# Layer 2 of a hybrid trunk: merge gates and merge products as separate units, and retention's first q and k between the grouped-query projections

## The chip, the cores and the metric

The kernel runs on one core of a Trainium2 chip. The metric is the device time of one execution in microseconds (us). Of three runs of the kernel before, the median is 1741.61 us (1741.46 to 1746.81). The engines are named PE (TensorE), DVE (VectorE), ACT (ScalarE), POOL (GpSimd) and SP (SyncE, which issues the DMAs).

## The reference

A trunk of two layers works on 512 latent tokens `x` and 256 context tokens `y`, 1024 channels wide. In each layer three branches read the same normalized input, each branch is gated, and a merge adds them up. Cut to what matters:

```python
def hybrid_layer(x, y, ..., need_ctx):                     # need_ctx only in layer 1
    hx = rms_norm(x, norm_w) * (1 + scale_x) + shift_x     # hy likewise
    rq, rk, rv, rg, nq, nk, nv, ng, gq, gk, gv, gg, mg = split_cols(hx @ w_in)
    # retention, 4 heads of 128, both directions, v used after its mean is taken off
    ret_x = head_group_norm(bidir_retention(...), ret_gn_w) * silu(rg)
    # neighbourhood attention, 8 heads of 64, windows of 8 rows x 16 columns, plus context keys
    na_x = neighbourhood_attention(...) * silu(ng)
    # grouped-query attention, 8 query heads on 2 key heads, rms norm and rope on q and k
    gqa_x = gqa_blocks(axial_rope(rms_norm(gq)), k_all, v_all) * silu(gg)
    g_ret, g_na, g_gqa = split(sigmoid(mg), 3)             # the merge gates, 1024 wide each
    m = g_ret * (ret_x @ w_ret_o) + g_na * (na_x @ w_na_o) + g_gqa * (gqa_x @ w_gqa_o)
    x = x + gate_x * (m @ w_out)
```

The same is done for the context in layer 1 alone. After layer 2 comes a last rms norm of `x`.

## The kernel before, in words

Everything is held transposed: channels on partitions, tokens along the free axis. Each fp32 operand is split into a high part and the remainder, so a product is three matmuls (`mm3`, L277 to L280): high by high, remainder by high, high by remainder. Normalized input is `hxh`, `hxl`, weights are `whi`, `wlo`. Weights arrive in tiles of 512 KB: `_load` (L252) issues the DMA to `raw` on SP, ACT casts each half to `whi` (L262), POOL subtracts it to get `wlo` (L264). The order of tiles is the list `stream`, filled from the plan at L1236.

A projection unit (`u_proj`) for one 128-wide block of output channels is 24 matmuls of 512 columns in layer 2 (8 input tiles by 3), and for units that also need the context tokens 24 more of 256 columns. `u_tok` makes v with tokens on partitions: 144 matmuls of 256 columns.

PE's order is written by hand. A `Unit` is a generator that emits one `mm3` per step. `run` emits units whole. `window` (L113) emits a branch's attention steps, and after each step as many `mm3` of filler units as the step's weight asks for; what is left over runs at the end of the window or, with `keep`, later. `defer(us, fn)` puts a small PE step (a transpose, a column sum) off until that many estimated microseconds of PE work have been emitted. The other engines are ordered by a scheduler that works from the same program; within an engine instructions run strictly in that order. PSUM is split into banks by tag: `pj` 2 (projections), `s` 2 (scores), `pt` 3 (transposes), `pv` 1.

One layer runs through these stages:

- Neighbourhood attention (NA) in four windows `p`, two heads each. Per head: four score steps (L595, L596, evicted by DVE with the bias, exponential on ACT, normalized by DVE and POOL), six transpose steps (L624; ACT casts the high part `ph`, L438, and DVE subtracts for `pl`, L439), six `pv` steps (L635 with `ph`, L636 with `pl`). Fillers are the next window's q and k and the window's gate `u_g`. Window 3 has no next window, so its filler is one gate alone.
- The intro to grouped-query attention (GQA): `u_k`, `u_v`, `u_q(0)`, merge 0 of the NA branch. k takes squares, a column sum (L225, L226), a wide inverse square root in three rounds of DVE and ACT (L218 to L220), a rope of four DVE instructions (L704 to L707), and ACT casts it to `gk` (L767). v is copied by ACT to `sg` (L779, 512 and then 256 tokens) and transposed on PE (L784).
- GQA in four windows `p`. Per window four units (two heads by two halves of the queries) of four score steps (L851, L852; DVE evicts to `p`, L853), exponential on ACT (L862), normalization by DVE and POOL (L867), three transpose steps (L875) and three `pv` steps (L887). Fillers: gate, next q, and merges 1 to 7 as listed in `GA`. The next q needs transposes of its squares `gsq` (L725), sums of them (L726), and a rope.
- The intro to retention (RET): tables `dt`, `E`, `C` by DVE and ACT, then `u_qk(0,"q")`, `u_qk(0,"k")`, `u_v(0)`, whose evictions take DVE four instructions per third (L990 to L996).
- RET in four windows, with merges of the GQA branch as fillers; then the merges of the RET branch and the out projection.

A merge for output block `d` (`u_merge`) is one unit: gate projection of 24 matmuls, a tanh on ACT into `mt`, then a product of 12 matmuls with the branch's gated output `gat`, which DVE multiplies into `m[d]` (L1104).

Of the kernel before, what the change touches and what calls it, by code (L numbers as in the profile page):

```python
# [20 lines left out]
NX = 512  # L21
# [18 lines left out]
def trunk_kernel(ctx: ExitStack, tc: tile.TileContext, xt, wcol, wv, adaw, wbr, wout, nabias, vecs,  # L40
# [197 lines left out]
    SQ = 100  # L238
    KLAG = 3.0
    Q0LAG = 2.0  # L240
# [251 lines left out]
    class NA:  # L492
# [189 lines left out]
    class GQA:  # L682
# [19 lines left out]
        def rope(self, t):  # L702
            sh = self.ap.tile([128, NX], F32, tag="sh", name="sh", bufs=1)
            nc.vector.stream_shuffle(out=sh, in_=t[:, :NX], mask=[(i + 16) % 32 for i in range(32)])  # L704
            nc.vector.tensor_tensor(t[:, :NX], t[:, :NX], self.cs[:, 0], op=ALU.mult)
            nc.vector.tensor_tensor(sh, sh, self.cs[:, 1], op=ALU.mult)
            nc.vector.tensor_tensor(t[:, :NX], t[:, :NX], sh, op=ALU.add)  # L707

        def stats_evac(self, t, w, ntok, done, lag):

            st = {}

            def ev(ps, o, n):
                if o == 0:
                    st["ss"] = self.ap.tile([128, 12], F32, tag="qss", name="qss", bufs=2)
                ss = st["ss"]
                sq = self.ap.tile([128, 512], F32, tag="sh", name="gsq", bufs=1)
                with tc.high_priority(SQ):
                    nc.scalar.activation(sq[:, :n], ps, AF.Square)
                nc.scalar.activation(t()[:, o:o + n], ps, AF.Copy, scale=w)  # L720

                def one():
                    pt = bank("pt")
                    for i in range(n // 128):
                        nc.tensor.transpose(pt[:, 128 * i:128 * i + 128], sq[:, 128 * i:128 * i + 128], ident)  # L725
                    nc.vector.tensor_reduce(ss[:, o // 64:(o + n) // 64], pt[:, :n].rearrange("p (t c) -> p t c", c=64),  # L726
                                            axis=AX.X, op=ALU.add)
                    if o + n == ntok:
                        done(ss[:, :ntok // 64])
                defer(lag, one)  # L730
            return ev

        def u_k(self):
            st = {}

            def ev(ps, o, n):
                ap = self.ap
                if o == 0:
                    st["kr"] = ap.tile([128, NT], F32, tag="qr", name="kr", bufs=1)
# [5 lines left out]
                sq = ap.tile([128, 512], F32, tag="sh", name="gsq", bufs=1)  # L745
                sh, sl = a[:, 0, c].bitcast(F32R), a[:, 1, c].bitcast(F32R)
# [6 lines left out]
                def one():  # L753
# [18 lines left out]
        def u_v(self):  # L772
            st = {}

            def ev(ps, o, n):
                if o == 0:
                    st["v"] = self.ap.tile([128, NT], F32, tag="sg", name="sg", bufs=1)
                vf = st["v"]
                nc.scalar.copy(vf[:, o:o + n], ps)  # L779

                def tr():
                    pt = bank("s")
                    for i in range(n // 128):
                        nc.tensor.transpose(pt[:, 128 * i:128 * i + 128], vf[:, o + 128 * i:o + 128 * i + 128], ident)  # L784
                    for i in range(n // 128):
                        v = self.V[:, o // 128 + i]
                        src = pt[:, 128 * i:128 * i + 128].rearrange("p (h d) -> p h d", h=2)
                        nc.scalar.copy(v[:, :, 0:64], src)
                        nc.vector.tensor_tensor(v[:, :, 64:128], src, f(v[:, :, 0:64]), op=ALU.subtract)
                defer(1.5, tr)  # L790
            return u_proj(ap_wcol[self.l][CT_GV], G_ALL, ev)

        def u_q(self, p):
            def get():
                if p not in self.qr:
                    self.qr[p] = self.ap.tile([128, NT], F32, tag="qr", name="qr", bufs=1)
                return self.qr[p]
# [124 lines left out]
    class RET:  # L922
        def __init__(self, l, g):
            self.l, self.g = l, g
            self.nq = NT if l == 0 else NX
            self.gq = G_ALL if l == 0 else G_LAT
            self.ot, self.sg = {}, {}

        def open(self):
# [33 lines left out]
        def u_qk(self, h, which):  # L963
            sc = 1.0 if which == "q" else float(np.float32(128.0) ** np.float32(-0.5))

            def ev(ps, o, n):
                if o == 0:
                    t = (self.ap.tile([128, NT], F32R, tag=which + "h", name=which + "h", bufs=1),
                         self.ap.tile([128, NT], F32R, tag=which + "l", name=which + "l", bufs=1))
                    setattr(self, which, t)  # L970
# [8 lines left out]
        def u_v(self, h):  # L979
            def ev(ps, tp):  # L980
                ap = self.ap
                if tp == 0:
# [93 lines left out]

    def u_merge(l, b, d, g, m, getpool):
        gq = G_ALL if l == 0 else G_LAT
        nq = NT if l == 0 else NX
        src = [ap_wcol[l][CT_MG + 8 * b + d]]  # L1080
        if d % 2 == 0:
            src.append(ap_wbr[l][b][d // 2])

        def gen(ws):
            if d % 2 == 0:
                wbr_now[0] = ws[1]
            t = getpool().tile([128, nq], F32, tag="mt", name="mt", bufs=1)

            def ev(ps, o, n):
                nc.scalar.activation(t[:, o:o + n], ps, AF.Tanh, scale=0.5)  # L1090
            yield from g_proj(ws[0], gq, ev)
            hi, lo = wbr_now[0][d % 2]
            if len(g) < 4:
                due(True)
            for o, n in gq:
                ps = bank("pj")
                for k in range(4):
# [10 lines left out]
                    yield 3 * n * NS  # L1108
        return Unit(nq * 36 * NS, src, gen)

    wbr_now = [None]

# [5 lines left out]
    def start_phase(na, first):  # L1118
# [47 lines left out]
    for l in range(DEPTH):  # L1166
# [30 lines left out]
        def open_m(l=l, m=m, mtp=mtp):  # L1197
# [3 lines left out]
            for d in range(8):  # L1201
                m[d] = mp.tile([128, nq], F32, tag="m", name="m", bufs=8)
            mtp["cm"] = pool(f"mt{l}")
            mtp["p"] = mtp["cm"].__enter__()
        do(open_m)
        do(gqa.open)
        mg = lambda b, d, g: u_merge(l, b, d, g, m, lambda mtp=mtp: mtp["p"])
        runs(gqa.u_k(), gqa.u_v(), gqa.u_q(0))
        MA = ((0, 1), (2, 3), (4, 5), (6, 7))
        GA = ((1, 2), (3, 4), (5,), (6, 7))  # L1210
        old = []
        for p in range(4):
            if p == 0:
                runs(mg(BR_NA, 0, g_na))
            do(lambda gqa=gqa, p=p: (due(True), gqa.split_q(p)))
            us = [gqa.u_g(p)] + ([gqa.u_q(p + 1)] if p < 3 else []) + [mg(BR_NA, d, g_na) for d in GA[p]]
            win(lambda gqa=gqa, p=p: gqa.steps(p), us, GLEAD, GKEEP[l][p], old)
# [6 lines left out]
        do(lambda ret=ret: ret.tables(0))  # L1224
        runs(ret.u_qk(0, "q"), ret.u_qk(0, "k"), ret.u_v(0))
        for h in range(4):
            us = [ret.u_g(h)] + [mg(BR_GQA, d, g_gq) for d in MA[h]]
# [4 lines left out]
        do(lambda ret=ret: (due(True), ret.close()))  # L1232
        plan.append(("end", l, m, mtp, g_rt))
# [6 lines left out]
    for e in plan:  # L1240
# [6 lines left out]
        elif e[0] == "end":  # L1247
            l, m, mtp, g_rt = e[1:]
            end_units[l] = [u_merge(l, BR_RET, d, g_rt, m, lambda mtp=mtp: mtp["p"]) for d in range(8)]
            add(end_units[l])  # L1250
            stream.extend(ap_wout[l][0] + ap_wout[l][1])

    def finish(l, m, mtp):
# [4 lines left out]
        mhl = {}  # L1258
        for d, u in enumerate(end_units[l]):
            run([u])  # L1260
            if l == 0:
# [222 lines left out]
```

## Time and profile before

| | |
|---|---|
| median of three runs | 1741.61 us |
| the profiled execution: its own time | 1744.02 us |
| its span in the trace, first to last instruction | 1742.2 us |
| granted TensorE clock, mean over the span | 0.993 |
| PE busy | 1665.9 us (96%), 9940 matmuls |
| weight loads (PEld), beside PE | 1439.5 us (83%) |
| DVE, ACT, POOL busy | 1056.7 (61%), 796.8 (46%), 556.4 us (32%) |
| DMA | 146.38 MB, mean 84 GB/s |

A matmul's end is modelled in the trace, and it overlaps the next one's start: what counts for PE's pace is the distance from start to start. An idle time in square brackets at a row's end is thus shorter than what PE lost there. The stages of layer 2 in the trace: NA's window 3 runs from 1143.2 to 1173.1 us, GQA's intro to 1208.3, its windows 0 to 3 to 1257.4, 1301.4, 1348.0 and 1388.4, RET's intro to 1419.4.

### The profile page before, as it was taken

The page shows a single profiled execution, that of the slowest core. Times are in us where ns is not written, and L with a number is a line of the kernel's source. Part 1 is how long each engine was busy: PE and PEld are TensorE (multiplying, and loading weights), DVE is VectorE, ACT ScalarE, POOL GpSimd, SP SyncE. Part 2 cuts the span into 40 slices and gives each one's busy share as a digit, 9 for nine tenths or more (in the row PEclk, how much of TensorE's full clock was granted, in tenths as well). Part 3 has the DMA queues.
Part 4 walks back from the last instruction along what each step waited for, and adds up shares of the span by engine and source line. Part 5 has one row for each costly group of instructions (what it writes and reads, how often), then busy time and mean ns, then how long its engine had stood idle before and what let it go on. Part 6 is the DMA issues. An engine that isn't in the chain of part 4 may idle for free. (4 is left out here: it accounts for less than half of the span.)

```text
span 1742.2 us, 26141 instructions
## 1 busy us (share of the span) xinstructions
PE 1665.9 (96%) x9940; PEld 1439.5 (83%) x9940; DVE 1056.7 (61%) x2201; ACT 796.8 (46%) x1570; POOL 556.4 (32%) x486
## 2 busy tenths in 40 slices
PE   6899999999999999999999999999999999999997
PEld 4778888888899889888887889877787897887786
DVE  6666567666654655565324766668677646555456
ACT  4455564555553443443223445654555544344342
POOL 1433332233233222322222343423333333243432
PEclk9999999999999999999999999999999999999998
DMA  8211111111111121214536521311111121122245
GB/s 317 80 51 56 58 49 49 37 49 37 37 60 49 49 61 37 63 50 157 203 133 206 171 97 47 99 49 61 49 58 52 60 73 61 61 76 70 91 136 160
DMA packets 43053, 146.38 MB, mean 84 GB/s; under 512 B 4912, under 2 KB 10160, under 8 KB 39856
## 3 DMA queue, kind: packets, MB, share of 16 engines
q1 hardware_dynamic: 42928, 144.72, 25.0%
q8 instruction: 78, 1.28, 0.3%
q14 instruction: 47, 0.39, 0.1%
HBM read 140.51 MB, written 4.19 MB: 83 GB/s over the span
## 5 line engine op out<-in xcount | busy, mean ns | idle before, releaser
L264 POOL TENSOR_TENSOR wlo<-raw,whi 128x512 fp32r<-128x512 f32 x345 | 457.3, 1330 | 972.3 <-ACT whi L262 923.6
L278 PE MATMUL pj<-hxh,whi 128*128 128x512 f32 (+1 forms) x1448 | 527.7, 364 | 9.8 <-DVE ql L974 3.9
L279 PE MATMUL pj<-hxl,whi 128*128 128x512 f32 (+1 forms) x1448 | 510.3, 352 | 1.1 <-DVE hxl L404 1.1
L280 PE MATMUL pj<-hxh,wlo 128*128 128x512 f32 (+1 forms) x1448 | 509.7, 352 | 0.0
L262 ACT CAST whi<-raw 128x512 fp32r<-128x512 f32 x376 | 231.4, 618 | 293.2 <-PE pj L279 214.8
L278 PEld LDWEIGHTS pj<-hxh,whi 128*128 128x128 f32 x1448 | 274.2, 189 | 43.1 <-DVE ql L974 5.8
L280 PEld LDWEIGHTS pj<-hxh,wlo 128*128 128x128 f32 x1448 | 273.9, 189 | 39.0
L279 PEld LDWEIGHTS pj<-hxl,whi 128*128 128x128 f32 x1448 | 274.9, 190 | 28.1 <-DVE hxl L404 2.2
L439 DVE TENSOR_TENSOR pl<-pt,ph 128x512 fp32r<-128x512 f32 (+2 forms) x208 | 126.7, 625 | 52.9 <-ACT ph L438 50.7
L278 PE MATMUL pj<-gat,whi 128*128 128x512 f32 (+1 forms) x416 | 144.6, 348 | 2.6 <-ACT gat L917 2.0
L279 PE MATMUL pj<-gat,whi 128*128 128x512 f32 (+1 forms) x416 | 142.4, 342 | 0.6 <-DVE gat L1271 0.3
L280 PE MATMUL pj<-gat,wlo 128*128 128x512 f32 (+1 forms) x416 | 142.0, 341 | 0.0
L438 ACT CAST ph<-pt 128x512 fp32r<-128x512 f32 (+2 forms) x208 | 107.6, 533 | 69.4 <-PE pt L624 29.4
L310 PE MATMUL pj<-whi,hxh 128*128 128x256 f32 x384 | 110.5, 288 | 3.1 <-DVE kz L427 2.3
L312 PE MATMUL pj<-whi,hxl 128*128 128x256 f32 x384 | 109.4, 285 | 0.0
L311 PE MATMUL pj<-wlo,hxh 128*128 128x256 f32 x384 | 109.4, 285 | 0.0
L278 PEld LDWEIGHTS pj<-gat,whi 128*128 128x128 f32 x416 | 79.2, 190 | 11.9 <-ACT gat L917 2.5
L862 ACT ACTIVATE p<-p,nm,rq 128x768 f32<-128x768 f32 x64 | 65.4, 1024 | 46.7 <-DVE nm L860 46.1
L280 PEld LDWEIGHTS pj<-gat,wlo 128*128 128x128 f32 x416 | 79.0, 190 | 9.4
L279 PEld LDWEIGHTS pj<-gat,whi 128*128 128x128 f32 x416 | 79.1, 190 | 8.9 <-DVE gat L1271 0.5
L853 DVE TENSOR_SCALAR_CACHE_REDUCE p<-s 128x384 f32<-128x384 f32 x128 | 69.0, 554 | 28.0 <-PE s L852 26.7
L1106 DVE SCALAR_TENSOR_TENSOR mt<-mt,pj 128x512 f32<-128x512 f32 (+1 forms) x48 | 28.6, 596 | 91.9 <-PE pj L280 91.3
(265 smaller groups left out, 2957.6 us busy)
## 6 DMA issues: line engine op xcount, KB each, us to landing
raw<-in_wcol_dram SPq DMA_DIRECT2D x116, 512.0 KB, 3.5
araw<-in_adaw_dram SPq DMA_DIRECT2D x24, 1024.0 KB, 6.4
raw<-in_wout_dram SPq DMA_DIRECT2D x32, 512.0 KB, 3.5
raw<-in_wbr_dram SPq DMA_DIRECT2D x24, 512.0 KB, 3.5
raw<-in_wv_dram SPq DMA_DIRECT2D x16, 512.0 KB, 3.5
bias<-in_nabias_dram SPq DMA_DIRECT2D x16, 384.0 KB, 3.1
x<-in_xt_dram SPq DMA_DIRECT2D x8, 384.0 KB, 6.0
xo<-in_xt_dram SPq DMA_DIRECT2D x8, 256.0 KB, 3.7
```

The lines of the kernel that those rows point to most:

```text
L262: nc.scalar.copy(hi, raw[:, c])
L264: lo_eng.tensor_tensor(lo, raw[:, c], f(hi), op=ALU.subtract)
L278: mm(ps, lhsT=sh, rhs=mh, start=start, stop=False)
L279: mm(ps, lhsT=sh, rhs=ml, start=False, stop=False)
L280: mm(ps, lhsT=sl, rhs=mh, start=False, stop=stop)
L310: mm(o, lhsT=sh[:, tok], rhs=hi, start=(k == 0), stop=False)
L311: mm(o, lhsT=sh[:, tok], rhs=lo, start=False, stop=False)
L312: mm(o, lhsT=sl[:, tok], rhs=hi, start=False, stop=(k == KT - 1))
L438: nc.scalar.copy(ph[:, :n], pt[:, :n])
L439: nc.vector.tensor_tensor(pl[:, :n], pt[:, :n], f(ph[:, :n]), op=ALU.subtract)
L853: nc.vector.tensor_scalar(P[:, jj, kk], s[:, :384], 1.0, -3.0e38, op0=ALU.mult, op1=ALU.max, accum_out=mx[:, i:i + 1])
L862: nc.scalar.activation(P[:, a], P[:, a], AF.Exp, bias=nm[:, a:a + 1], scale=rqe[:, 2 * hf + a:2 * hf + a + 1], accum_out=sm[:, a:a + 1])
```

## The change

`u_merge` becomes two units: `u_mgate` (24 matmuls, tanh) and `u_mprod` (12 matmuls, multiply). In layer 1 each pair stands where the merge stood, so that PE, DVE, ACT, POOL and SP keep their order there. In layer 2:

- NA's window 3 gets the gates of merges 0, 1 and 2 as fillers, behind its own gate; `mt` has four buffers in place of one.
- GQA's intro runs `u_k`, RET's first q, `u_v`, `u_q(0)`, RET's first k, and then the products 0, 1 and 2. The tiles of RET's first q, k and v come from a pool of their own that is open from there.
- GQA's windows get merges (3, 4), (5), (6) and none, in place of (1, 2), (3, 4), (5) and (6, 7); window 3 gets RET's first v.
- RET's intro runs merge 7 alone, in place of q, k and v.
- The tags `sh` (rope's shuffle and `gsq`) and `qr` have two buffers in place of one; the column sum of k is put off by 4.5 instead of 3.0, the transposes of v by 2.5 instead of 1.5.

```diff
-    KLAG = 3.0
+    KLAG = (3.0, 4.5)
+    VTLAG = (1.5, 2.5)
...
-            sh = self.ap.tile([128, NX], F32, tag="sh", name="sh", bufs=1)
+            sh = self.ap.tile([128, NX], F32, tag="sh", name="sh", bufs=1 + self.l)
...
-                sq = self.ap.tile([128, 512], F32, tag="sh", name="gsq", bufs=1)
+                sq = self.ap.tile([128, 512], F32, tag="sh", name="gsq", bufs=1 + self.l)
...
-                defer(KLAG, one)
+                defer(KLAG[self.l], one)
...
-                defer(1.5, tr)
+                defer(VTLAG[self.l], tr)
...
-                    self.qr[p] = self.ap.tile([128, NT], F32, tag="qr", name="qr", bufs=1)
+                    self.qr[p] = self.ap.tile([128, NT], F32, tag="qr", name="qr", bufs=1 + self.l)
...
-    def u_merge(l, b, d, g, m, getpool):
+    def u_mgate(l, b, d, getpool):
+        gq = G_ALL if l == 0 else G_LAT
         nq = NT if l == 0 else NX
...
+            t = merge_t[b, d] = getpool().tile([128, nq], F32, tag="mt", name="mt", bufs=MTB[l])
 
             def ev(ps, o, n):
                 nc.scalar.activation(t[:, o:o + n], ps, AF.Tanh, scale=0.5)
             yield from g_proj(ws[0], gq, ev)
+        return Unit(nq * 24 * NS, [ap_wcol[l][CT_MG + 8 * b + d]], gen)
+
+    def u_mprod(l, b, d, g, m):
...
+            t = merge_t.pop((b, d))
...
-        return Unit(nq * 36 * NS, src, gen)
+        return Unit(nq * 12 * NS, [ap_wbr[l][b][d // 2]] if d % 2 == 0 else [], gen)
+
+    merge_t = {}
+    MTB = (1, 4)
...
+            if (l, p) == (1, 3):
+                us += [mgate(BR_NA, d) for d in EARLY[l]]
...
+            runs(gqa.u_k(), ret.u_qk(0, "q"), gqa.u_v(), gqa.u_q(0), ret.u_qk(0, "k"))
         MA = ((0, 1), (2, 3), (4, 5), (6, 7))
-        GA = ((1, 2), (3, 4), (5,), (6, 7))
+        GA = (((1, 2), (3, 4), (5,), (6, 7)), ((3, 4), (5,), (6,), ()))[l]
...
+            elif p == 0:
+                runs(*[mprod(BR_NA, d, g_na) for d in EARLY[l]])
...
+            if l == 1 and p == 3:
+                us.append(ret.u_v(0))
...
-        runs(ret.u_qk(0, "q"), ret.u_qk(0, "k"), ret.u_v(0))
+        if l == 0:
+            runs(ret.u_qk(0, "q"), ret.u_qk(0, "k"), ret.u_v(0))
+        else:
+            runs(*mg(BR_NA, (7,), g_na))
```

Three places show how it moves instructions; numbers behind a name tell buffers apart.

On ACT, in GQA's intro of layer 2 before: `gk10` and `gk11` are the keys cast from the finished `kr`, `sg` is v's copy, `ks` a step of k's inverse square root, `whi` a weight cast.

```order
L218 ACTIVATE ks_12325<-kr_r_12410 128x256
L788 CAST gv_12287<-s_12457 128x2x64
L262 CAST whi_12492<-raw_12486 128x512
L779 COPY sg_12445<-pj_12447 128x256
L788 CAST gv_12287<-s_12503 128x2x64
L262 CAST whi_12539<-raw_12533 128x512
L767 CAST gk10_12283<-kr_12323 64x768
L767 CAST gk11_12284<-kr_12323 64x768
```

The same place on ACT in the changed kernel.

```order
L770 CAST gk10_12397<-kr_12437 64x768
L263 CAST whi_12688<-raw_12686 128x512
L770 CAST gk11_12398<-kr_12437 64x768
L791 CAST gv_12401<-s_12619 128x2x64
L782 COPY sg_12598<-pj_12600 128x256
L263 CAST whi_12692<-raw_12686 128x512
L791 CAST gv_12401<-s_12662 128x2x64
```

The copy of v's last 256 tokens, for which PE's second transpose of v waits, stood ahead of both key casts and now stands behind them.

On DVE, before, in GQA's window 0 of layer 2, ahead of the score eviction `p`: `sh` and `qr` belong to the rope of the next q, `rs_t` and `rq` to its inverse square root.

```order
L706 TENSOR_TENSOR sh_12877<-sh_12877,cs_12281 128x512
L210 SCALAR_TENSOR_TENSOR rs_t_12865<-rs_t_12865,rs_x_12864 128x8
L439 TENSOR_TENSOR pl_12900<-pt_12894,ph_12899 128x512
L211 SCALAR_TENSOR_TENSOR rq_12863<-rs_t_12865,rq_12863 128x8
L707 TENSOR_TENSOR qr_12811<-qr_12811,sh_12877 128x512
L209 TENSOR_TENSOR rs_t_12865<-rq_12863 128x8
L853 TENSOR_SCALAR p_12906,mx_12907<-s_12911 128x384
```

The same place in the changed kernel, from the rope's shuffle (L707) to its last instruction (L710); the eviction `p` follows six rows further on.

```order
L707 STREAM_SHUFFLE sh_13097<-qr_13031 128x512
L708 TENSOR_TENSOR qr_13031<-qr_13031,cs_12395 128x512
L709 TENSOR_TENSOR sh_13097<-sh_13097,cs_12395 128x512
L729 TENSOR_REDUCE qss_13028<-pt_13077 128x8
L867 RECIPROCAL rc_12997<-sm_12996 128x2
L434 TENSOR_TENSOR ot_12845<-pv_13002,ot_12845 64x256
L206 TENSOR_SCALAR rs_x_13084<-qss_13028 128x8
L870 TENSOR_SCALAR p_12993<-p_12993,rc_12997 128x768
L207 TENSOR_SCALAR rq_13083<-rs_x_13084 128x8
L440 TENSOR_TENSOR pl_13071<-pt_13065,ph_13070 128x512
L209 TENSOR_TENSOR rs_t_13085<-rq_13083 128x8
L710 TENSOR_TENSOR qr_13031<-qr_13031,sh_13097 128x512
```

The shuffle and the two multiplies of the rope have moved ahead of the sum `qss`; before, all four stood behind it.

On PE, before, at the start of GQA's window 1 of layer 2: the last scores of the first two units and what stands between them and the first transpose of `p` (L875).

```order
L851 MATMUL s_13198<-gk10_12283,q_13112 128x384
L852 MATMUL s_13198<-gk20_12285,q_13112 128x384
L278 MATMUL pj_13156<-hxh_9576,whi_13020 128x512
L279 MATMUL pj_13156<-hxl_9577,whi_13020 128x512
L280 MATMUL pj_13156<-hxh_9576,wlo_13021 128x512
L278 MATMUL pj_13156<-hxh_9578,whi_13024 128x512
L279 MATMUL pj_13156<-hxl_9579,whi_13024 128x512
L280 MATMUL pj_13156<-hxh_9578,wlo_13025 128x512
L278 MATMUL pj_13156<-hxh_9580,whi_13024 128x512
L279 MATMUL pj_13156<-hxl_9581,whi_13024 128x512
L280 MATMUL pj_13156<-hxh_9580,wlo_13025 128x512
L875 MATMUL pt_13218<-ident_90,p_13133 128x128 x4
```

The same place in the changed kernel.

```order
L854 MATMUL s_13411<-gk10_12397,q_13322 128x384
L855 MATMUL s_13411<-gk20_12399,q_13322 128x384
L854 MATMUL s_13415<-gk10_12397,q_13322 128x384
L855 MATMUL s_13415<-gk20_12399,q_13322 128x384
L279 MATMUL pj_13380<-hxh_9574,whi_13331 128x512
L280 MATMUL pj_13380<-hxl_9575,whi_13331 128x512
L281 MATMUL pj_13380<-hxh_9574,wlo_13332 128x512
L878 MATMUL pt_13429<-ident_90,p_13353 128x128 x4
```

From the window's first score to this transpose there stood 18 filler matmuls between the eight score steps; now there are 9.

## Rows read from the trace of the kernel before

**Rows 1.** Table by stretch: length, busy PE, PEld, DVE, ACT, POOL, granted clock, DMA.

```profile
1155.60:1173.10 17.50, 15.51 (x84) 11.66 (x83) 13.14 (x32) 10.48 (x25) 5.19 (x5) 1.00 0.17 61
1257.40:1301.40 44.00, 42.91 (x239) 35.97 (x238) 32.61 (x89) 25.75 (x49) 16.93 (x13) 1.00 0.16 52
1348.00:1388.40 40.40, 39.79 (x225) 33.85 (x224) 24.88 (x70) 22.48 (x44) 15.44 (x12) 1.00 0.20 65
1240.00:1243.40 3.40, 3.40 (x11) 3.11 (x12) 2.26 (x7) 1.48 (x4) 0.77 (x1) 0.50 0.00 0
```

**Rows 2.** Groups of PE instructions, 1155.6 to 1173.1: count, then busy, mean, idle.

```profile
L624 PE MATMUL pt<-ident,pb 128*128 128x128 f32 x20 | 4.0, 272 | 0.0
```

**Rows 3.** Timeline of PE, NA's window 3: start, duration, instruction, [idle before, its releaser].

```profile
1155.65 0.27 PE L624 MATMUL pt<-ident,pa 128*128 128x128 f32 x1
1155.76 0.27 PE L624 MATMUL pt<-ident,pb 128*128 128x128 f32 x1
...
1172.92 0.38 PE L636 MATMUL pv<-pl,v 128*128 128x256 f32 x1 [0.41 <-DVE pl L439]
```

**Rows 4.** Timeline of PE, GQA's intro: k's column sum, and four steps that waited.

```profile
1181.51 0.40 PE L225 MATMUL pt<-ks,blk 128*128 128x512 f32 x1
...
1189.44 0.66 PE L784 MATMUL s<-ident,sg 128*128 128x128 f32 x4 [0.53 <-ACT sg L779]
1194.02 0.44 PE L784 MATMUL s<-ident,sg 128*128 128x128 f32 x2 [0.74 <-ACT sg L779]
1201.75 0.66 PE L725 MATMUL pt<-ident,gsq 128*128 128x128 f32 x4 [1.14 <-ACT gsq L719]
1212.19 0.41 PE L851 MATMUL s<-gk,q 128*128 128x384 f32 x1 [0.91 <-DVE q L427]
```

**Rows 5.** Timeline of DVE, POOL and ACT, GQA's intro: end of k's chain.

```profile
1188.62 0.42 DVE L220 SCALAR_TENSOR_TENSOR kr_r<-ks,kr_r 128x256 f32<-128x256 f32 x1
...
1191.13 1.33 POOL L264 TENSOR_TENSOR wlo<-raw,whi 128x512 fp32r<-128x512 f32 x1 [7.47 <-ACT whi L262]
1191.22 1.51 DVE L220 SCALAR_TENSOR_TENSOR kr_r<-ks,kr_r 128x256 f32<-128x256 f32 x1
...
1193.60 0.36 ACT L779 COPY sg<-pj 128x256 f32<-128x256 f32 x1
...
1196.60 1.77 DVE L707 TENSOR_TENSOR kr<-kr,sh 128x512 f32<-128x512 f32 x1
...
1198.41 1.69 ACT L767 CAST gk<-kr 64x768 fp32r<-64x768 f32 x2 [2.08 <-DVE kr L707]
```

**Rows 6.** Timeline of DVE and PE, GQA's window 0, second half.

```profile
1230.79 0.69 DVE L726 TENSOR_REDUCE qss<-pt 128x8 f32<-128x512 f32 x1 [1.26 <-PE pt L725]
...
1235.29 0.73 DVE L704 STREAM_SHUFFLE sh<-qr 128x512 f32<-128x512 f32 x1
...
1239.98 0.69 PE L851 MATMUL s<-gk,q 128*128 128x384 f32 x1 [2.06 <-DVE p L853]
...
1240.79 0.63 PE L278 MATMUL pj<-hxh,whi 128*128 128x512 f32 x1
```

**Rows 7.** Timeline of PE and POOL, start of GQA's window 1.

```profile
1259.97 0.39 PE L280 MATMUL pj<-gat,wlo 128*128 128x512 f32 x1
1260.19 0.33 PE L851 MATMUL s<-gk,q 128*128 128x384 f32 x1
1260.36 0.34 PE L852 MATMUL s<-gk,q 128*128 128x384 f32 x1
...
1266.41 1.33 POOL L867 TENSOR_SCALAR p<-p,rc 128x768 f32<-128x768 f32 x1 [4.20 <-DVE rc L864]
...
1267.48 0.76 PE L875 MATMUL pt<-ident,p 128*128 128x128 f32 x3
```

**Rows 8.** Groups of DVE instructions: RET's intro, then one of all of layer 2.

```profile
L946 DVE TENSOR_SCALAR dt<-tabs,nlg 128x896 f32<-128x896 f16 x1 | 1.8, 1759 | 0.0
...
L996 DVE TENSOR_TENSOR vl<-vc,vh 128x512 fp32r<-128x512 f32 x6 | 4.1, 691 | 4.2 <-ACT vh L995 4.2
```

More of the change, by code (lines that the diff above doesn't have):

```diff
@@ L738, in ev @@
                 if o == 0:
-                    st["kr"] = ap.tile([128, NT], F32, tag="qr", name="kr", bufs=1)
+                    st["kr"] = ap.tile([128, NT], F32, tag="qr", name="kr", bufs=1 + self.l)
                     st["a"], st["b"] = (ap.tile([128, 2, NT], F32, tag="p", name="ks", bufs=2) for _ in range(2))
@@ L744, in ev @@
                 kr, a, b = st["kr"], st["a"], st["b"]
-                sq = ap.tile([128, 512], F32, tag="sh", name="gsq", bufs=1)
+                sq = ap.tile([128, 512], F32, tag="sh", name="gsq", bufs=1 + self.l)
                 sh, sl = a[:, 0, c].bitcast(F32R), a[:, 1, c].bitcast(F32R)
@@ L927, in __init__, with open_first @@
             self.ot, self.sg = {}, {}
+            self.first = None
+        def open_first(self):
+            self.first_cm = pool(f"rq{self.l}")
+            self.first = self.first_cm.__enter__()
         def open(self):
@@ L967, in ev @@
                 if o == 0:
-                    t = (self.ap.tile([128, NT], F32R, tag=which + "h", name=which + "h", bufs=1),
-                         self.ap.tile([128, NT], F32R, tag=which + "l", name=which + "l", bufs=1))
+                    ap = self.ap if self.first is None else self.first
+                    t = (ap.tile([128, NT], F32R, tag=which + "h", name=which + "h", bufs=1),
+                         ap.tile([128, NT], F32R, tag=which + "l", name=which + "l", bufs=1))
                     setattr(self, which, t)
@@ L980, in ev @@
             def ev(ps, tp):
-                ap = self.ap
+                ap = self.ap if self.first is None else self.first
                 if tp == 0:
@@ L1202, in open_m @@
                 m[d] = mp.tile([128, nq], F32, tag="m", name="m", bufs=8)
-            mtp["cm"] = pool(f"mt{l}")
-            mtp["p"] = mtp["cm"].__enter__()
         do(open_m)
+        if l == 0:
+            do(open_mt)
+        else:
+            do(ret.open_first)
         do(gqa.open)
-        mg = lambda b, d, g: u_merge(l, b, d, g, m, lambda mtp=mtp: mtp["p"])
-        runs(gqa.u_k(), gqa.u_v(), gqa.u_q(0))
+        mg = lambda b, ds, g: [u for d in ds for u in (mgate(b, d), mprod(b, d, g))]
+        if l == 0:
+            runs(gqa.u_k(), gqa.u_v(), gqa.u_q(0))
+        else:
+            runs(gqa.u_k(), ret.u_qk(0, "q"), gqa.u_v(), gqa.u_q(0), ret.u_qk(0, "k"))
         MA = ((0, 1), (2, 3), (4, 5), (6, 7))
-        GA = ((1, 2), (3, 4), (5,), (6, 7))
+        GA = (((1, 2), (3, 4), (5,), (6, 7)), ((3, 4), (5,), (6,), ()))[l]
         old = []
         for p in range(4):
-            if p == 0:
-                runs(mg(BR_NA, 0, g_na))
+            if p == 0 and l == 0:
+                runs(*mg(BR_NA, (0,), g_na))
+            elif p == 0:
+                runs(*[mprod(BR_NA, d, g_na) for d in EARLY[l]])
             do(lambda gqa=gqa, p=p: (due(True), gqa.split_q(p)))
-            us = [gqa.u_g(p)] + ([gqa.u_q(p + 1)] if p < 3 else []) + [mg(BR_NA, d, g_na) for d in GA[p]]
+            us = [gqa.u_g(p)] + ([gqa.u_q(p + 1)] if p < 3 else []) + mg(BR_NA, GA[p], g_na)
+            if l == 1 and p == 3:
+                us.append(ret.u_v(0))
             win(lambda gqa=gqa, p=p: gqa.steps(p), us, GLEAD, GKEEP[l][p], old)
@@ L1231, in trunk_kernel @@
                 runs(ret.u_qk(h + 1, "q"), ret.u_qk(h + 1, "k"), *([ret.u_v(2)] if h == 1 else []))
-        do(lambda ret=ret: (due(True), ret.close()))
+        do(lambda ret=ret: (due(True), ret.close(), ret.first is not None and ret.first_cm.__exit__(None, None, None)))
         plan.append(("end", l, m, mtp, g_rt))
@@ L1248, in trunk_kernel @@
             l, m, mtp, g_rt = e[1:]
-            end_units[l] = [u_merge(l, BR_RET, d, g_rt, m, lambda mtp=mtp: mtp["p"]) for d in range(8)]
-            add(end_units[l])
+            end_units[l] = [[u_mgate(l, BR_RET, d, lambda mtp=mtp: mtp["p"]), u_mprod(l, BR_RET, d, g_rt, m)] for d in range(8)]
+            for us in end_units[l]:
+                add(us)
             stream.extend(ap_wout[l][0] + ap_wout[l][1])
@@ L1258, in finish @@
         mhl = {}
-        for d, u in enumerate(end_units[l]):
-            run([u])
+        for d, us in enumerate(end_units[l]):
+            run(us)
             if l == 0:
```

27 lines of the change are left out of this document (18 added, 9 removed).

## The prediction

> **What bounds the kernel now.** I read the table by stretch first [rows 1]. In each stage of layer 2 around the change PE is busy for nearly all of the time, at a granted clock of 1.00, and DVE for 62 to 75% of it. So only time in which PE stands still, or is slow, can be won, and DVE is what PE waits for. Filler that is moved costs PE nothing and saves it nothing by itself; its worth is what it covers where it goes, and what it uncovers where it leaves.
>
> The second view is the pace on PE's timeline: starts of 512-column matmuls lie 0.22 to 0.23 us apart, 384 columns 0.17 [rows 7], a transpose 0.11 [rows 3]. The modelled ends overlap the next start by some 0.16 us, so a wait in brackets costs that much more than it says. Layer 1 keeps its order on all engines, so its time stands. Layer 2 issues the same matmuls, DVE and ACT work and DMAs in another order. So all terms are waits.
>
> **The parts, in order of time.** A minus is a gain.
>
> *A, end of NA's window 3.* In the 17.50 us of the stretch [rows 1] PE issues 36 transposes (20 of them read `pb` [rows 2]; 36 x 0.11 = 4.0), 31 matmuls of 512 columns (15 of filler, 8 scores, 8 pv; 31 x 0.23 = 7.1), 8 of 384 (1.4) and 8 of 256 columns (at half the pace of 512, 0.9): 13.4 us. It lost 4.1 us. The rows that wait name `pl` [rows 3]: with little left to lay between, a pv step comes right behind its transposes, and its ACT cast and DVE subtraction show. Afterwards 72 gate matmuls (16.6 us) lie between these steps. DVE has 13.1 us of work here and ACT 10.5 [rows 1], far less than the longer stage, so the waits should go, except those at the edges. I take 0.9 left: **-3.2**. Bounds: 0, if the chain from `pt` to `pl` stays as exposed, and -4.1.
>
> *B, GQA's intro.* Four waits of PE stand in rows 4: 0.53, 0.74, 1.14 and 0.91, with 0.16 each 3.9 us. With 24 matmuls each of retention's q and k laid between, they are covered but for some 0.2: -3.7. A new wait comes at the second transpose of v. PE would reach it 16.4 us after k's column sum starts: two sums (0.46), 15 matmuls of 512 columns (3.45), two sums of 256 (0.24), 27 of 512 (6.2), 18 of 256 (2.2), the first transposes (0.4), 6 of 256 and 12 of 512 (3.5). But the copy of v's last 256 tokens stands behind both key casts on ACT, and these wait for the finished `kr`. Before, `kr` was finished at 1196.60 + 1.77 = 1198.37, 16.9 us after the sum's start at 1181.51 [rows 4, 5]; two casts with a weight cast between (1.69 + 0.6), a small cast of v (0.3) and the copy (0.36) follow: 19.8. With one of the three slow DVE steps of rows 5 (1.1 us each) met only half, I take 19.2, a wait of 2.8. Bounds: 0.1 (none of the three) and 5.1 (a fourth, and a weight cast more). A wait of 2.06 us in rows 6 was followed by matmuls at 0.42 instead of 0.23 apart, at a granted clock of 0.50 (that is 1.2 GHz) for 3.4 us [rows 1]: half of it, 1.7 us, is lost. The wait of 1.14 was not. I charge 1.4 for the clock. Sum: -3.7 + 2.8 + 1.4 = **+0.5**, bounds -3.6 and +3.1.
>
> The slow steps are seen in rows 5: the same DVE instruction took 0.42 us, and 1.51 when POOL's subtraction for `wlo` (1.33) started 0.09 before it: 1.09 more. The Trainium skill ("SBUF — State Buffer", section "SBUF: two separate sides") says that VectorE and GpSimd share one pair of ports as an exclusive lock, the loser blocked for the other's whole instruction. By that rule the step would have taken 1.24 + 0.42 = 1.66 us; the trace shows 1.51, so nearly the whole. With 0.15 more for each of three such meetings the wait would be 0.5 longer and the time 1742.5.
>
> *C, GQA's window 0.* PE waits 2.06 (+0.16) for an eviction of scores, and the clock falls behind it [rows 6, 1]: 2.2 + 1.7. Ahead of that eviction DVE worked off the rope of the next q; its shuffle could not start before `qss` had freed the one buffer of `sh`. With two buffers the shuffle and both multiplies, about 0.7 us each as the instruction of the same size in rows 6, move ahead, some 2.1 us. They fill the 1.26 us in which DVE stood idle before `qss` [rows 6], and push `qss` and the next reciprocal back by about 0.5. So the eviction comes 1.5 us earlier; 0.7 is left of the wait, no lower clock, and 0.1 is lost at the reciprocal: **-3.1**. Bounds: -0.8 (the eviction 0.8 earlier, the clock falls all the same) and -3.9.
>
> *D, GQA's windows 1 and 2.* Window 1 loses one merge, 36 matmuls, 8.2 us of cover. First: from the first score to the first transpose of `p`, 7.29 us before (1260.19 to 1267.48 [rows 7]), PE had 16 matmuls of 384 columns and 18 of filler (2.75 + 4.1 = 6.9); it has 9 of filler now, 4.8 us. `p` is ready when POOL has normalized it, about 7.3 us after the first score as now [rows 7], up to 7.8 if the fifth eviction gets ahead of the maximum. So 2.5 to 3.0 are lost where 0.4 were: +2.1 to +2.6, I take 2.4. Second: between the transposes of `gsq` and the scores of window 2 stand 19 PE instructions or 4.8 us now, 20 us before. What DVE and ACT have to do there (sum 0.69, shuffle 0.73, three rope steps of 0.7, cast and split of q 0.6 + 0.7 to 1.0, and `pl` between) comes to 6.1: +1.4, bounds 0 and 2.3. Third: the rest of the window has 32 us of DVE work [rows 1] in 36 us of PE work in place of 44; with DVE that full the kind of wait that A removes comes up here; I take +0.7 (0.5 to 1.0). Fourth: these waits are in pieces below 2 us, so I charge 0.4 for the clock (0 to 1.7). Sum **+4.9**, bounds 3.0 and 8.0.
>
> *E, GQA's window 3.* In place of two merges lies `u_v(0)`, the same PE time but 6.7 us of DVE work (three evictions of 2.1 to 2.3, from 0.69 a step [rows 8]) against 1.4. DVE then has 30 of 40 us [rows 1], as window 1 before. **+0.8**, bounds 0 (its slack takes it) and 3.
>
> *F, RET's intro.* It falls from 31 to 8.3 us of PE work. On DVE the multiply of merge 7 stands ahead of the tables; `dt` takes 1.76 us [rows 8], then come its second step, ACT's `E` and an addition, so the first scaled score is ready 13.6 us after GQA's end. PE has its lead fillers and first scores until about 13: **+0.5**, bounds 0 and 2.
>
> Where A to F count an edit at nothing (the doubled `mt`, the SP queue's reordered weight loads, the split of the unit itself), the cover is the same matmuls at the same pace: a load lands well ahead of the second tile in line, and a late one would show as PE waiting for `whi`.
>
> **Sum**: -3.2 + 0.5 - 3.1 + 4.9 + 0.8 + 0.5 = +0.4 us against the profiled execution's 1744.02, or 1744.4. That run was 2.4 us above the median of the runs shown, 1741.61; against that it is 1742.0. A measurement of this kernel can tell about 0.3%, 5.2 us, from no change.
>
> **Rivals.**
>
> *The new waits are covered, faster.* If the scheduler's order costs less than its chains suggest, above all if `kr` is done early enough that v's copy is on time (B: -3.7), and D comes at 3.0, E and F at nothing: -3.2 - 3.7 - 3.1 + 3.0 = -7.0, 1734.6. For it: the slow DVE steps hit by chance, and slack of half a microsecond at each step would do. Against it: both key casts stand ahead of the copy in ACT's order, and rows 5 price that.
>
> *The new waits each bring the clock down, slower.* The mechanism is C's, moved: a PE that stands 2 us drops to the lower clock for 3.4 us. At v's second transpose (B at +2.8), at the first transpose of `p` and at window 2's first score (D at 8.0) it would cost 1.7 each time. With A at -3.2, C at -3.1, E at +2 and F at +1.5: +8.0, 1749.6. It decides from waits of about 2 us, by rows 4 and 6. For it: D's first wait is estimated at 2.5. Against it: PE works in pieces between, held at the score banks. The Trainium skill ("TensorE: Matmul & The Clock Gate", section "HAM oscillation — how this bites in real kernels") tells of the same: idle gaps between bursts put the array back at its lower clock. The trace agrees behind 2.06 us, and not behind 1.14.
>
> *The change doesn't do what it says.* The gates laid into NA's window cover nothing, since casts and subtractions only queue up longer: A at 0, +3.6, 1745.2. Against it: DVE and ACT would be under 45% busy there.
>
> **Chances.** The forecast, with the third rival that ends within 0.3% too, 0.57; its own range 1737 to 1746.8. The first rival, and its neighbours past -0.3%, 0.26; the second 0.17. The range takes in both rivals' times, as a tenth may lie beyond either end: 1734 to 1749.6.
>
> **What would show it.** A: no waits on `pl` in NA's window 3. B: PE waiting at the second transpose of v for `sg`, some 3 us, and matmuls 0.42 apart behind it. C: 1.00 clock through window 0. D: a wait of 2 to 3 us at the first transpose of `p` in window 1 and one before window 2's scores. It would be wrong if v's transpose doesn't wait, or if window 1 takes under 38 us (44 less 8.3 is 35.7, and D adds 3.5 or more).

## The result, and the profile after

The changed kernel takes 1755.67 us (median of five runs, 1750.75 to 1758.15), the kernel before 1743.09 beside it; the ratio estimated from these runs is 1.0064, its 95% interval 1.0048 to 1.0081. It is slower, by more than the range of the prediction (1737 to 1746.8) allowed for. The profiled execution is the fastest of the five, 1750.75. A second profiled execution of the same kernel (label e8 below) took 1756.64 and is nearer to the median, so both are read here.

First, the table by stretch of the kernel before, between marks that both kernels have: the last pv step of NA's window 2, NA's last pv step, the first score of each GQA window, the last pv step of GQA. The columns are those of [rows 1].

```profile
1152.80:1172.90 20.10, 18.13 (x97) 13.78 (x95) 14.46 (x34) 13.16 (x32) 6.70 (x6) 1.00 0.18 64
1172.90:1212.20 39.30, 35.96 (x184) 29.83 (x184) 31.59 (x62) 18.89 (x39) 10.83 (x8) 1.00 0.17 54
1212.20:1260.20 48.00, 45.15 (x241) 38.12 (x242) 33.84 (x89) 25.43 (x50) 18.80 (x14) 0.96 0.16 55
1260.20:1304.20 44.00, 42.91 (x238) 35.98 (x237) 32.48 (x89) 25.20 (x48) 16.73 (x13) 1.00 0.15 49
1304.20:1348.70 44.50, 42.26 (x235) 35.57 (x234) 31.87 (x87) 25.04 (x48) 15.59 (x12) 1.00 0.17 53
1348.70:1388.30 39.60, 38.99 (x221) 33.19 (x220) 24.12 (x69) 21.75 (x43) 15.44 (x12) 1.00 0.19 62
```

The same six stretches of the changed kernel, first profile:

```profile
1152.45:1184.65 32.20, 32.20 (x166) 26.79 (x165) 15.93 (x34) 17.79 (x39) 12.96 (x11) 1.00 0.17 56
1184.65:1239.30 54.65, 50.47 (x261) 42.37 (x260) 37.85 (x68) 22.99 (x46) 18.66 (x14) 1.00 0.23 77
1239.30:1284.60 45.30, 43.46 (x242) 36.44 (x241) 33.40 (x87) 25.53 (x49) 17.70 (x13) 1.00 0.19 59
1284.60:1327.50 42.90, 35.20 (x203) 29.23 (x201) 29.20 (x80) 22.63 (x44) 12.92 (x10) 1.00 0.11 37
1327.50:1375.20 47.70, 44.30 (x235) 37.07 (x236) 34.22 (x94) 25.16 (x48) 15.43 (x13) 0.96 0.14 45
1375.20:1415.10 39.90, 39.16 (x290) 36.86 (x289) 26.73 (x74) 20.14 (x39) 11.51 (x9) 1.00 0.09 28
```

And its GQA windows 1 and 2 in the second profile:

```profile
1287.80:1333.70 45.90, 38.19 (x202) 31.83 (x200) 29.54 (x80) 22.81 (x44) 12.88 (x10) 0.93 0.11 35
1333.70:1381.50 47.80, 44.28 (x235) 36.96 (x236) 34.17 (x94) 25.14 (x48) 15.43 (x12) 0.96 0.14 45
```

Take from each length the filler that was moved (in these traces a 512-column matmul takes 0.228 us from start to start, one of 256 columns 0.118).

- NA: +12.1, of it 15.7 for 69 of the 72 gate matmuls, since three more of the window's filler than before run behind its last pv step: 3.6 gained.
- Intro: +15.35, of it 14.5 for retention's q and k and those three: 0.9 lost.
- Window 0: the same filler, 2.7 gained.
- Window 1: -1.1 where 36 matmuls (8.2) left: 7.1 lost, 10.1 in the second profile.
- Window 2: the same filler, 3.2 lost.
- Window 3: 0.1 lost.
- From there to the end of the span: 353.9 before, 333.9 after, where 22.2 left: 2.2 lost.

Together that is 7.2 us in the first profile and 9.9 in the second. The spans differ by 6.8 and 12.7; the rest, -0.4 and 2.8, lies ahead of 1152 us, where the order is the same.

Window 1 is the stage to look at: PE busy 35.2 of 42.9 us, against 42.9 of 44.0. The timeline of PE in the changed kernel has the waits:

```profile
1214.62 0.44 PE L787 MATMUL s<-ident,sg 128*128 128x128 f32 x2 [2.35 <-ACT sg L782]
1220.96 0.44 PE L728 MATMUL pt<-ident,gsq 128*128 128x128 f32 x2 [1.11 <-ACT gsq L722]
1292.79 0.30 PE L878 MATMUL pt<-ident,p 128*128 128x128 f32 x1 [1.74 <-DVE p L870]
1306.63 0.39 PE L890 MATMUL pv<-pl,gv 128*128 128x256 f32 x1 [1.43 <-DVE pl L440]
1327.50 0.44 PE L854 MATMUL s<-gk,q 128*128 128x384 f32 x1 [1.77 <-DVE q L428]
1432.47 0.51 PE L279 MATMUL pv<-ph,vh 128*128 128x512 f32 x1 [2.42 <-ACT ph L439]
```

The first is the new wait at v's second transpose, the third the one at window 1's first transpose of `p`, the fifth the one before window 2's scores; all three stand where they were forecast. The fourth is one of window 1's waits at pv steps. The second answers to the wait at 1201.75 in [rows 4], which was to go and did not. The last, in RET's window 0, has its source on SP and DVE:

```profile
1423.48 0.42 SPq L942 DMA_DIRECT2D tabs<-in_cst_dram  x1
...
1427.76 0.69 DVE L955 TENSOR_SCALAR dt<-tabs,nlg 128x896 f32<-128x896 f16 x1 [1.96 <-DMA tabs<-in_cst_dram]
```

The tables' load is issued 8 us after GQA's last pv step, behind weight loads in SP's queue, and DVE waits 1.96 us for it. Before, it was issued 2.5 us ahead of that step (1388.30), and `dt` [rows 8] found it landed:

```profile
1385.76 0.43 SPq L933 DMA_DIRECT2D tabs<-in_cst_dram  x1
```

### The profile page after: what moved, and what is told of

Read it like the earlier page. It is cut to its first block, busy times and chain, and to the rows that moved or that the text cites. A ratio compares the mean times of both kernels' runs of the same rounds, so it can differ in the third digit from the quotient of the medians.

```text
span 1749.0 us, 26138 instructions
## 1 busy us (share of the span) xinstructions
PE 1661.4 (95%) x9940; PEld 1436.0 (82%) x9940; DVE 1061.0 (61%) x2201; ACT 797.5 (46%) x1570; POOL 556.1 (32%) x486
## 4 chain that ended last, share of the span: by engine, by line
PE 72%; DVE 17%; ACT 5%; issue 3%; DMA 1%; POOL 1%; SPq 0%; DVEq 0%; ACTq 0%; POOLq 0%
PE pj L279 16%; PE pj L280 16%; PE pj L281 16%; PE pv L890 2%; PE pj L311 2%; PE pj L313 2%; PE pj L312 2%; PE pt L878 2%; DVE pl L440 1%; PE pt L627 1%; PE s L854 1%; DVE pf L220 1%; PE s L855 1%; PE pt L345 1%; DVE vc L219 1%
## 5 line engine op out<-in xcount | busy, mean ns | idle before, releaser
L865 ACT ACTIVATE p<-p,nm,rq 128x768 f32<-128x768 f32 x64 | 65.4, 1023 | 51.7 <-DVE nm L863 51.1
```

The lines of the kernel that those rows point to most:

```text
L865: nc.scalar.activation(P[:, a], P[:, a], AF.Exp, bias=nm[:, a:a + 1], scale=rqe[:, 2 * hf + a:2 * hf + a + 1], accum_out=sm[:, a:a + 1])
```

## The experiments

Ratios are to the kernel before in runs beside each other, with their 95% intervals. One theory (W) is that the time follows PE's waits at the places that the change uncovers; its rivals are named with each run. Diffs are cut to the lines that matter.

**Only the doubled buffers.**

```diff
-  ... tag="sh", bufs=1   (and gsq, kr, qr)
+  ... tag="sh", bufs=1 + self.l
```

> The kernel before with only the tags sh and qr doubled in layer 2; nothing else is moved by hand. Theory W (the time follows the waits of PE that each part takes away or uncovers): the 2.06 us wait for a score eviction in GQA's window 0 shrinks below 1 us and the lower clock behind it is gone, window 0 takes 45 to 46 us instead of 48.0 from first score to first score, the time falls by 2 to 4 us. Rival (the gain in window 0 came from the other moves, since window 0 of the changed kernel has other merges and starts later): wait and window stay as before, no difference.

0.9978 (0.9968 to 0.9987), 1741.0 us. Window 0 of this kernel:

```profile
1213.50:1259.30 45.80, 43.93 (x241) 36.53 (x242) 34.42 (x89) 25.43 (x50) 19.30 (x14) 1.00 0.17 58
```

2.2 us less and no stretch of lower clock; the wait of 2.06 us is gone, the longest left in the window is 0.61. W holds, and the buffers alone are a gain.

**Gates early, retention's projections back in their place.**

```diff
-            runs(gqa.u_k(), ret.u_qk(0, "q"), gqa.u_v(), gqa.u_q(0), ret.u_qk(0, "k"))
+            runs(gqa.u_k(), gqa.u_v(), gqa.u_q(0))
-        ((3, 4), (5,), (6,), ())
+        ((3, 4), (5,), (6,), (7,))
```

> The changed kernel with retention's first q, k and v back in RET's intro, the three gates early, merges (3,4), (5), (6), (7) in GQA's windows, and the two lags as before. Theory W: NA's window 3 keeps its gain of 4.3 us and window 0 its 2.7, windows 1 and 2 keep their loss of 8 to 10 us since window 1 has one merge, window 3 has one merge instead of two and loses 1 to 3, RET's intro is as before: 1744 to 1750. Rival R (the loss comes from retention's projections laid early, which load DVE and ACT and the weight stream): as fast as the gains alone, 1735 to 1738.

The two lags are as before, too. 1.0089 (1.0074 to 1.0105), 1759.71 us. Rival R falls: with retention's projections back, windows 1 and 2 take 44.6 and 46.2 us, as lossy as in the change. But W's range is missed by 10 us. Window 3, now with one merge, takes 36.3 where 39.6 - 8.2 = 31.4 would be even: 4.9 lost, and I had expected 1 to 3. And there is a wait that I had not seen, between the products 0 to 2 with no projection between them; behind it matmuls are 0.43 us apart for 3.4 us:

```profile
1225.99 0.68 PE L279 MATMUL pj<-gat,whi 128*128 128x512 f32 x1 [4.34 <-DVE m L1120]
```

**Retention's projections early, no early gates.** Merge 0 stands ahead of window 0 again, merges 6 and 7 go to RET's intro.

```diff
-        EARLY = ((), (0, 1, 2))
+        EARLY = ((), ())
-        ((3, 4), (5,), (6,), ())
+        ((1, 2), (3, 4), (5,), ())
```

> The changed kernel without early gates: merge 0 ahead of window 0 and (1,2), (3,4), (5), none in the windows, as before in windows 0 to 2; retention's first q and k in GQA's intro and v in window 3 as in the change; merges 6 and 7 in RET's intro. Theory W: no gain in NA's window 3 (its 4 us of waits are back), intro +1 to +2 by the wait at v's second transpose, window 0 -2.7, windows 1 and 2 as before or 1 us off, RET's intro 8 us longer covers the late table load: 1740 to 1745. Rival R (retention's early projections carry the loss): 1750 or more.

1.0010 (1.0001 to 1.0020), 1745.92 us, 1 us above W's range. Windows 0 to 2 take 45.7, 43.8 and 43.9 us: with two merges in window 1 nothing is lost there. The wait at v's second transpose (2.31 us) is there, as expected. The one in RET's window 0 (2.42) is there too, against what I had written: in the intro with two merges the load is issued later as well, 16.5 us after GQA's last pv step instead of 8.4, in SP's queue behind a weight load both times, so it moves back with the work that was to cover it. W holds for the windows and not for that stage. R falls as the carrier of the loss, but the early projections are not free: beside the doubled buffers alone (0.9978 against the same runs of before) this kernel is 0.3%, some 5 us, slower.

**Tables loaded early.**

```diff
-            nc.sync.dma_start(out=tabs, in_=cst16)          # in RET.open
+            nc.sync.dma_start(out=self.tabs[:, 0:896], in_=cst16[:, 0:896])   # in open_first; tpos likewise
-    MTB = (1, 4)
+    MTB = (1, 3)
```

With four buffers of `mt` the whole table would leave GQA's tiles 65.4 KB per partition where they need 67.5. So two of its three parts are loaded, the ones that layer 2 uses, and `mt` has three buffers.

> The changed kernel with retention's tables of positions (the two parts that layer 2 uses) loaded at the start of GQA instead of after its end; the merge tag has three buffers in place of four to make room. Theory L (late load): dt no longer waits 1.96 us for the DMA, the wait of 2.42 us at RET's first pv step falls below 1 us, and the time is 2 to 3 us below the changed kernel's, 0.45 to 0.55% above before. Rival (DVE's order, with the multiply of merge 7 and the ones ahead of the tables, sets the start of the scores, as I priced it blind): the wait stays above 2 us, no gain, 0.64% above before.

1.0036 (1.0023 to 1.0048): 0.28% below the changed kernel, somewhat more than theory L's 0.1 to 0.2%; the intervals of the two kernels touch. The wait of 2.42 is gone, one of 0.77 is left:

```profile
1430.75 0.51 PE L280 MATMUL pv<-pl,vh 128*128 128x512 f32 x1 [0.77 <-DVE pl L440]
```

The load was what held the tables; DVE's order, by which I had priced this stage, was not. The waits that stood there, 2.42 and 0.65, are less than the 4.9 us that the ratio fell by; what the rest comes from is not shown.

**One merge from window 0 to window 1.**

```diff
-        ((3, 4), (5,), (6,), ())
+        ((3,), (4, 5), (6,), ())
```

> The changed kernel with merge 4 moved from GQA's window 0 to window 1: (3), (4,5), (6), none. Theory V (a window of GQA needs two merges of cover beside its gate and q; the second one is nearly free, some 1 us of its 8.2): window 1, 42.9 us in the changed kernel, takes 43.5 to 45, and window 0, 45.3 us, takes 43.5 to 45 as well; the waits of 1.74 at the first transpose of p and 1.77 before the next window's scores move from window 1 to window 0; the time stays within 2 us of the changed kernel. Rival (the loss belongs to window 1, by the doubled buffers' other order or the place of the rope): window 1 takes about 51 us and keeps its waits, window 0 about 37.

1.0006 (0.9996 to 1.0016): 0.58%, 10 us, better than the change. The profile is of the slowest of its ten runs, 1750.36 where the median is 1745.0. Its windows 0 to 2:

```profile
1242.30:1284.00 41.70, 35.87 (x205) 30.07 (x204) 30.98 (x86) 23.37 (x45) 13.46 (x10) 1.00 0.12 39
1284.00:1327.80 43.80, 42.72 (x239) 36.10 (x239) 31.66 (x89) 25.14 (x48) 16.61 (x13) 1.00 0.19 61
1327.80:1371.70 43.90, 42.23 (x236) 35.44 (x235) 31.57 (x87) 25.16 (x48) 15.53 (x12) 1.00 0.15 49
```

Neither theory had this time. Window 1 is sound again (43.8) and a wait of 1.65 us now stands at the first transpose of `p` in window 0, as V said, but the one before the next window's scores has not come along. Window 2, which has the same filler in both kernels, is sound too. But window 0 with one merge loses only 4.6 us (41.7 against 45.3 - 8.2), where window 1 with one lost 7.1 and window 2 behind it 3.2 more. So a missing merge is not the same loss everywhere.

**What sets window 1 apart: filler held back.** `GKEEP` leaves filler of a window over for the next: in layer 2, 3.2 us in window 0, 6.5 in window 1, 2.0 in window 2. The change took a merge from window 1 and left the 6.5.

```diff
-    GKEEP = (..., (3.2, 6.5, 2.0, 0.0))
+    GKEEP = (..., (3.2, 2.0, 2.0, 0.0))
```

> The changed kernel with one number changed: the filler held back to the end of GQA's window 1 in layer 2 is 2.0 instead of 6.5 (it was set when the window had two merges). The same 60 matmuls of filler, spread earlier; the transposes of gsq come 18 matmuls earlier before window 2's scores. Theory K (window 1's loss is not the missing merge itself but that 6.5 of its 19 us of filler are held back, so that steps stand bare and the next q is late): windows 1 and 2 together, 90.6 us in the changed kernel's first profile, take 85 to 87, the waits before window 2's scores (1.77, 0.73, 1.03) go, no stretch of lower clock there: 4 to 8 us below the changed kernel, 0.2 to 0.45% above before. Rival V (cover is what is missing, wherever it is laid): windows 1 and 2 gain under 2 us, 0.6% above before.

(The filler of the window is 84 matmuls, not 60: gate, q and one merge.) 1.0027 (1.0016 to 1.0037), 0.4% below the changed kernel. Windows 1 and 2:

```profile
1288.30:1331.10 42.80, 39.50 (x221) 32.98 (x220) 31.48 (x88) 24.35 (x47) 14.53 (x11) 1.00 0.15 45
1331.10:1374.10 43.00, 38.06 (x218) 32.29 (x217) 31.82 (x88) 23.73 (x46) 14.43 (x11) 1.00 0.13 42
```

18 matmuls have gone from window 2 to window 1 (203 to 221, 235 to 218), window 1 is no longer than in the changed kernel (42.8 and 42.9), and window 2 is 4.7 shorter: 85.8 us in place of 90.6 and 93.7. The waits before window 2's scores fall to one of 0.48, and no lower clock is left in either. Theory K holds for about half of the loss: 44.0 - 8.2 + 44.5 = 80.3 us would be even, so 5.5 of 10.3 or 13.4 are left. Window 2 now waits 1.83 at its own first transpose of `p`. That the rest is the missing cover is not shown.

**Both of these repairs.** The arrangement of units is the change's.

> The same with the tables loaded early (merge tag with three buffers): the change's arrangement of units untouched, only a kept amount and a load repaired. Theory K: the sum of both repairs, 0.3% for the load and 0.2 to 0.45% for the kept filler: 1741 to 1746, within 0.2% of before. Rival V: 0.3 to 0.35% above before, as with the early tables alone.

1.0006 (0.9997 to 1.0015), 1745.45 us: the sum, as K said. One number and an early load turn a loss of 11 us into none that can be measured.

**The second profile.** The changed kernel again.

> The changed kernel once more, for a second profile. Theory P (the first profile, 5 us below the median of its runs, had by chance no stretch of lower clock at 1004 us, where the profile of before has 6.8 us of it; the waits are the same in every run): the same waits at the same places within 0.1 us, and a time between 1752 and 1758 with more stretches at a granted clock of 0.50. Rival (other runs have longer waits, as of a DMA): stalls differ by more than 1 us at some place after 1143 us.

1756.64 and 1756.22 us. From 1143 us to RET's window 0, the first profile's waits above 0.6 us are there within 0.1 us, but for that at `gsq`, which is gone. Further on three waits of 0.91 us for retention's `ql` are gone as well. So no wait is longer by more than 0.1 us; by the letter `gsq`, 1.11 us shorter, meets the rival's sign, but in the slower execution. Five stretches of lower clock lie in the changed stages, where the first profile has one (in window 2) and before one [rows 1]; the first two of them, and the wait ahead of the first:

```profile
1217.81 0.44 PE L787 MATMUL s<-ident,sg 128*128 128x128 f32 x2 [2.41 <-ACT sg L782]
```

```profile
1219.00:1222.40 3.40, 3.40 (x10) 2.60 (x9) 3.29 (x5) 0.22 (x2) 0.96 (x1) 0.51 0.39 112
1297.60:1301.00 3.40, 3.40 (x14) 2.91 (x13) 2.15 (x4) 2.28 (x4) 2.25 (x2) 0.50 0.00 0
```

The same wait of 2.35 us at 1214.62 left the clock at 1.00 in the first profile. Two of the five lie in window 1 and make it 45.9 us instead of 42.9. Theory P holds; of the 5.9 us between the two profiles, 3.15 are gathered ahead of the change.

**The transposes of v later.**

```diff
-    VTLAG = (1.5, 2.5)
+    VTLAG = (1.5, 5.5)
```

> The changed kernel with the transposes of v in layer 2 put off by 5.5 instead of 2.5: the second one stands 12 matmuls (2.8 us of PE) later. Theory W: the wait of 2.35 us at it falls below 0.8, no lower clock follows it, window lengths stay; 2 to 4 us below the changed kernel, 0.42 to 0.55% above before. Rival (the next wait, for the squares gsq 6 us later, takes over what is freed): gsq's wait of 1.1 us grows to 3 and the time stays at 0.65 to 0.7% above before.

1.0050 (1.0030 to 1.0069): within W's range, and not to be told from the changed kernel's 1.0064, so the time does not decide. The trace does. The wait at v shrinks to less than 0.6 us, and the next takes it over:

```profile
1223.77 0.33 PE L728 MATMUL pt<-ident,gsq 128*128 128x128 f32 x1 [3.00 <-ACT gsq L722]
```

The intro keeps its length (54.9 us, 54.65 in the change). The rival is right. What holds the squares is seen on ACT:

```profile
1222.43 0.27 ACT L791 CAST gv<-s 128x128 fp32r<-128x128 f32 x1 [3.44 <-DVE gv L792]
1223.11 0.60 ACT L722 ACTIVATE gsq<-pj 128x512 f32<-128x512 f32 x1
```

ACT works off k's casts, v's casts and q's squares in this order, and a cast of v stands still for 3.44 us (3.63 in the changed kernel) until DVE has subtracted an earlier `gv`, which stands behind DVE's split of the keys. So it is this chain over DVE and ACT that sets the squares' time, and a wait taken away at one of its consumers is met at the next. This fits the second profile, where the lower clock at 1219.0 cost nothing in the intro (54.7 us): there the wait for `gsq` is gone.

**Three repairs: swap, tables, later transposes.**

> The changed kernel with three repairs together: merge 4 in window 1 instead of 0, tables loaded early (merge tag with three buffers), v's transposes put off by 5.5. Theory W (the loss is the sum of these three places and the lower clock behind them, each of its own): swap 10, tables 3, transposes 2 to 3 below the changed kernel's 1756: 1740 to 1743, 0 to 0.25% below before. Rival (the repairs free the same time, since a wait removed is met again at the next one): no better than the swap alone, 1744 to 1746.

0.9993 (0.9984 to 1.0003), 1742.33 us. It lies in W's range, but it is only 0.13% below the swap alone, with overlapping intervals, where the measured gains of tables and transposes (0.28 and 0.14%) would give 0.4%. The wait for `gsq` is 3.01 us as with the later transposes alone, and the profile of window 0 shows 43.2 us, with a stretch of lower clock, where the swap had 41.7.

**Another filler for NA's window 3.** Retention's first q and k go there; the merges and retention's v stay where they were before. The doubled buffers and the early tables are in it, too.

```diff
-                us += [mgate(BR_NA, d) for d in EARLY[l]]
+                us += [ret.u_qk(0, "q"), ret.u_qk(0, "k")]
```

> Retention's first q and k, not the merge gates, fill NA's window 3; everything from GQA's intro on in the order of before (merge 0 ahead of window 0, merges (1,2), (3,4), (5), (6,7) in the windows, retention's first v in RET's intro), sh and qr doubled, tables loaded early. Theory W: NA's window 3 gains 4.0 us, the doubled buffers 3.6 with their clock, windows 1 and 2 keep their cover, RET's intro has 17 us of v over the tables: 7 us faster than before, 1735 to 1738. Rival (q and k bring evictions by DVE into NA's window 3, which the gates' tanh on ACT does not, and the waits for pl stay): 1740 to 1742.

0.9963 (0.9951 to 0.9975), 1737.54 us (1734.92 to 1739.5): faster than both kernels and as W said. Beside the doubled buffers alone (0.9978) the intervals overlap, so how much of it is due to the new filler is read from the stage: NA's stretch takes 29.8 us with PE busy throughout, 9.7 more than before for 13.4 us of filler, so 3.7 are gained; windows 0 to 2 take 45.8, 43.7 and 43.9:

```profile
1153.30:1183.10 29.80, 29.80 (x166) 25.36 (x165) 17.02 (x36) 16.59 (x37) 10.03 (x9) 1.00 0.13 42
```

## Why the prediction was wrong

- *A, NA's window 3.* Right: 3.6 gained, 3.2 forecast, and no wait on `pl` is left. The rival that the gates cover nothing falls.
- *B, intro.* The new wait is as forecast (2.35 + 0.16 against 2.8). The sum, 0.9 lost against 0.5, was close in part by luck: the wait for `gsq` was struck off as covered, and 1.11 us of it stayed, since ACT's squares now stood behind casts of v that waited 3.63 us for DVE; and the 1.4 charged for the clock was not due in the first profile.
- *C, window 0.* Right: 2.7 gained, 3.1 forecast, 2.2 by the buffers alone.
- *D, windows 1 and 2.* The step that failed by its size: +4.9 forecast, upper bound 8.0; it was 10.3 in one profile and 13.4 in the other. "First", 2.4, was 3.0: 8.21 us from the first score to the first transpose of `p` (1284.58 to 1292.79), though 9 filler matmuls fewer stand in them than in the 7.29 before. "Second", 1.4, was 1.9 (1.77 + 0.16). "Third: the rest of the window", 0.7, was what is left of window 1's 7.1, that is 2.2. Window 2 lost 3.2, and for it the sum had no more than a share of the 0.4 for the clock: its two waits for evictions, 0.73 and 1.03, were in no term, and one stretch of lower clock fell into it. I had counted the filler that left, and taken the rest as spread over the window, when 6.5 us of it are held back to the next; with 2.0 held back 4.8 to 7.9 us are won back, and the 5.5 left are near the 4.9.
- *The clock.* I charged 1.8 us in all for stretches of 1.7 each. The second profile has five in the changed stages; the two in window 1 made it 3.0 longer, the one in the intro nothing. The second rival named the mechanism and three of the places, but put 1749.6 on it; the low end of the runs is near there, the median 6 above it.
- *E, window 3.* Right: 0.1 lost, 0.8 forecast, bounds 0 and 3.
- *F, RET's intro.* The step that failed is "Where A to F count an edit at nothing ... the SP queue's reordered weight loads": the tables' load is no weight, is issued late, and has no cover when the intro is 8 us long. F was +2.2 to the end of the span, not +0.5, with waits of 2.42 and 0.65 in RET's window 0; loading the tables early won 0.28%.

## What to carry to other kernels

A number that holds filler back belongs to the list of filler it was set for: when a unit is taken out of a window, count what is left within the window, not what left it. When a stage is emptied of matmuls, look for the loads that it covered, not only the instructions. And a stage whose end is set by a chain over two engines in fixed order gained nothing here from moving one of that chain's consumers.

## What was not expected of the hardware

The granted clock is not a function of the length of the wait ahead of it: at one place and in one order, a wait of 2.41 us was followed by 3.4 us at 0.51, and one of 2.35 us in another execution by none, while one of 2.06 us in the kernel before was followed by 3.4 us at 0.50 [rows 1, 6]. So a wait near 2 us may cost more than itself in one run and not in the next. The changed kernel's runs lie between 1750.75 us, at a mean clock of 0.995, and 1758.15, at 0.988. That its new waits make it scatter more is not shown: 19 runs of the kernel before lie between 1739.6 us, at 0.997, and 1747.45, at 0.991.
